# One-hot rows of the second keys stored token by token in the stage that builds the gate table

## The chip, the cores and the metric

The kernel runs on one core of a Trainium2 chip. The metric is the device time of one execution in microseconds (us), lower is better. Engines are named as in the profile: PE (matmuls) and PEld (its weight loads), DVE, ACT, POOL and SP (which only starts DMAs here).

## The reference

One layer of a residual block on 1024 tokens of width 1024, all float32: a mixer (gated delta rule and a linear recurrence), cross attention to 256 memory tokens, and a feed-forward part (PEER) that picks, for every token and each of 8 heads, the 16 best of 128 x 128 experts by the sum of two key scores. Cut to what matters here:

```python
def reference(x, mem, ...):
    x = x + hybrid_mixer(rmsnorm(x, norm_mix_w[0]), ...)
    x = x + memory_cross_attention(rmsnorm(x, norm_xattn_w[0]), rmsnorm(mem, norm_mem_w[0]), ...)
    x = x + peer_ffn(rmsnorm(x, norm_ffn_w[0]), ...)   # 128 (head, rank) slots per token:
    return rmsnorm(x, norm_final_w)                    # first key, second key, gate
```

What the changed stage computes: for each of 512 tokens the 128 x 128 table gate[second key, first key]. A token has 128 slots (8 heads x 16 ranks), each with a first key, a second key and a gate. The table is the product over the slots of the one-hot rows of the second keys with the one-hot rows of the first keys, these multiplied by the gates.

## The kernel before, in words

The tokens are treated in two ways. For 512 of them (D0 = 256 to 767) all 16384 experts are computed densely, and the gate table is multiplied in. For the other 512 each chosen expert's row is fetched from memory by POOL (line 1130) and worked into the token by DVE: 1024 row steps for 4 blocks of 128 tokens, a ring of 6 row buffers (tile `rb`). These steps are put between the other instructions by `Paced`, which counts estimated PE time; so DVE carries a stream of 1.2 us steps all the time.

The program runs in this order: mixers and attention (0 to about 1350 us in the trace), the gate stage (`gates`, from 1352 to 1821 us), and the dense part (from there to the end). The gate stage of the first 256 tokens runs beside the last attention unit and its key search; the order of all instructions on every engine is fixed when the program is written out, by estimates of each engine's time.

Gate stage, lines 942 to 996: the keys and gates of the tokens are transposed into `e1T`, `e2T` and `gtT` ([128 slots, tokens]). `gated(t0)` makes the one-hots of four tokens: DVE writes `o1` (first keys, bf16) and `o2` (second keys, float32, lines 963 and 966); ACT multiplies `o1` by the gates into `og` (tile `ohg`, four instructions). `products` does one float32 matmul per token with `o2` as weights and `og` as the moving operand (line 975; in the profile `gd<-ohg,oh`, two weight loads and two matmuls per token), ACT copies the result to `stage` (line 980) and after 16 tokens starts the DMA of 1 MB to the table `gd` in DRAM. `o2`, `og` and `stage` have two buffers each. The weights of one matmul are read as

```python
o2 = p.tile([128, 128, 4], F, name="oh2", bufs=2)     # [slot, key, token]
pe.matmul(ps[:, t, :], o2[:, :, t], og[:, t, :], start=True, stop=True)
```

so the 128 columns of one token's weights lie 4 floats (16 bytes) apart.

Of the kernel before, what the change touches and what calls it, by code (L numbers as in the profile page):

```python
# [8 lines left out]
F = mybir.dt.float32  # L9
BF = mybir.dt.bfloat16  # L10
FR = mybir.dt.float32r
I32 = mybir.dt.int32
U32 = mybir.dt.uint32
AF = mybir.ActivationFunctionType
# [3 lines left out]
D = 1024  # L18
# [4 lines left out]
D0 = T                      # the tokens that go by all experts; the others go by their experts' rows  # L23
# [26 lines left out]
def block_kernel(ctx: ExitStack, tc: tile.TileContext, a):  # L50
# [3 lines left out]
    written = {}                # by tile: when which part of it is written, by the estimate  # L54
# [17 lines left out]
    class Engine:  # L72
        """An engine, and an estimate of when it is through with what it got so far."""
# [25 lines left out]
    class Paced(Engine):  # L99
        """The tensor engine, with steps of the stream of rows put between its instructions."""  # L100
# [29 lines left out]
    early = gat.tile([128, NROW + 2, D], FR, name="rb")   # until the rows come  # L130
# [9 lines left out]
    # ---------------------------------------------------------------- constants  # L140
    identf = consts.tile([128, 128], F, name="identf")
    identb = fc.tile([128, 128], BF, name="identb")
    triu = fc.tile([128, 128], F, name="triu")          # [t, i] = t <= i
    ones = fc.tile([128, 128], F, name="ones")
    negm = fc.tile([128, 128], BF, name="negm")         # [j, i] = -1e30 where i < j
    iota16 = consts.tile([128, 16], BF, name="iota16")
    # masks of the block recursion: W = (T X) o (I - M_s); M_s[r, c] = 1 where r // s is odd
    # and c // s = r // s - 1 (the first one transposed)
# [53 lines left out]
    lpar = ld("lpar", (128, 4, 4))                          # conv_b, ba, bx, lambda  # L202
# [9 lines left out]
    # ---------------------------------------------------------------- helpers  # L212
    def rsqrt(v, n, name):
        """1/sqrt(v) for a positive [128, n] tile: a bit guess and Newton's steps."""
        ti = small.tile([128, n], I32, name=name + "i")
        y = small.tile([128, n], F, name=name + "y")
        t = small.tile([128, n], F, name=name + "t")
        dve.tensor_scalar(ti, v.bitcast(I32), 1, None, op0=OP.logical_shift_right)
        dve.tensor_scalar(y.bitcast(I32), ti, -1.0, 1597463007.0, op0=OP.mult, op1=OP.add)
        for _ in range(3):  # L220
            dve.tensor_mul(t, y, y)
            dve.scalar_tensor_tensor(t, t, -0.5, v, op0=OP.mult, op1=OP.mult)
            dve.scalar_tensor_tensor(y, t, 1.5, y, op0=OP.add, op1=OP.mult)
        return y

    def softplus(x, n, name):
        """max(x, 0) + log1p(exp(-|x|)), the log by its atanh series."""
        e = small.tile([128, n], F, name=name + "e")
        d = small.tile([128, n], F, name=name + "d")
        z2 = small.tile([128, n], F, name=name + "z")  # L230
        act.activation(e, x, AF.Abs)
        act.activation(e, e, AF.Exp, scale=-1.0)
        dve.tensor_scalar(d, e, 2.0, None, op0=OP.add)
        dve.reciprocal(d, d)
        dve.tensor_mul(e, e, d)
        dve.tensor_mul(z2, e, e)
        dve.tensor_scalar(d, z2, 1.0 / 19.0, None, op0=OP.mult)
        for k in (17, 15, 13, 11, 9, 7, 5, 3):
            dve.scalar_tensor_tensor(d, d, 1.0 / k, z2, op0=OP.add, op1=OP.mult)
        dve.scalar_tensor_tensor(d, d, 1.0, e, op0=OP.add, op1=OP.mult)  # L240
        dve.tensor_scalar(e, x, 0.0, None, op0=OP.max)
        dve.scalar_tensor_tensor(d, d, 2.0, e, op0=OP.mult, op1=OP.add)
        return d
# [8 lines left out]
    def wload(src):  # L252
        """A piece of weights: 1024 rows x 128 columns, [128, 8, 128]."""
        w = wp.tile([128, D], F, name="w", bufs=3)
        sp.dma_start(w, src)
        return c8(w)

    def norm(X, nb, Y, junk):
        """RMS of token-major tiles, to Y."""
# [9 lines left out]
    class Both:  # L269
        """Two tiles [128, 4, T] as one of 8."""  # L270
# [6 lines left out]
    class Pair:  # L277
        """A float32 operand as two float32r parts, for the time in which the gathered rows' memory
        is free; tmp: a place for [128, T] of products."""
# [3 lines left out]
    def low(i):  # L283
        """Memory of the rows, [128, 8, T]."""
        return early[:, 2 * i:2 * i + 2, :].rearrange("p s (c t) -> p (s c) t", c=D // T)

    def transposed(hT, Y, nb, wcol):
        """Token-major tiles to [d, chunk, tok], by the weights."""
# [30 lines left out]
    def proj_T(wname, j, hT, n):  # L319
        """[128 columns, n tokens] of the product with one 128-column tile of weights."""  # L320
# [17 lines left out]
    def proj(wname, j, lhs, nb, b0=0):  # L338
        """The token-major products [128 tokens, nb blocks, 128 columns]."""
# [18 lines left out]
    # ---------------------------------------------------------------- once: masks, gates' constants  # L358
# [18 lines left out]
    # ---------------------------------------------------------------- once: memory keys, values  # L377
# [26 lines left out]
    # ---------------------------------------------------------------- the mixer, T tokens  # L404
# [9 lines left out]
    def mixer(fp, t0, qkv):  # L414
        def conv(ps, ti, w, out, bias=0.0):
            """Causal 4-tap convolution along the tokens of one channel tile."""
# [16 lines left out]
        # a, b: token-major  # L433
# [25 lines left out]
        # q, k, v: channel-major, convolved, silu  # L459
# [12 lines left out]
        def side():  # L472
            # z: token-major, 2 silu(z)
# [8 lines left out]
            # RG-LRU: channel-major  # L482
            for j in range(4):
# [17 lines left out]
                # t = tanh(|log a| / 2): a = (1 - t) / (1 + t), sqrt(1 - a^2) = 2 sqrt(t) / (1 + t);  # L501
                # 1 / (1 + t) = (1 + exp(log a)) / 2, with a step of Newton's
# [6 lines left out]
                dve.scalar_tensor_tensor(rc, nw, 2.0, rc, op0=OP.subtract, op1=OP.mult)     # -1 / (1 + t)  # L509
# [13 lines left out]
        def out(b0, b1):  # L523
            """x1 = x + y W_out of some blocks."""
# [11 lines left out]
        # gated delta rule  # L536
# [17 lines left out]
        def prepare(b):  # L554
            """What a chunk needs of its decays and keys before its own steps."""
# [34 lines left out]
        for b in range(NB):  # L590
# [15 lines left out]
            if b == NB - 1 and t0 + T < S:  # L606
                load_x(qkv, t0 + T)             # keys and values of this pass are done with
# [101 lines left out]
            def normed(b, tok, o, rq):  # L709
                so = small.tile([128, 4], F, name="g_so")  # L710
                sq_sum(o, so)
                # o is short of the factor rq: rms(rq o) = rq o / sqrt(rq^2 mean(o^2) + eps)
# [15 lines left out]
                act.activation(qkv[:, 0:4, tok], py, AF.Copy, scale=gnw)    # q of these tokens is done with  # L728
# [24 lines left out]
    done = {}                           # x1, by its first token  # L753
    read, chosen = set(), set()         # ends of the tokens whose x2 is read, whose experts are chosen

    # ---------------------------------------------------------------- cross attention and keys
    def attend(fp, t0, nb, KT, VM):
# [52 lines left out]
        # PEER's keys  # L810
# [60 lines left out]
    def select(p, keep, s12, i12, row):  # L871
        """The 16 best of each head's sums. A pair (i, j) of the sorted lists can be among
        them only when (i + 1)(j + 1) <= 16; those all lie in: row 0 (16), rows 1-7 (j < 8),
        rows 8-15 (j = 0), kept in the order of the full table."""
# [24 lines left out]
        # position -> (i, j)  # L899
# [6 lines left out]
        dve.tensor_sub(t1, pf, low)                                     # 8 (pos // 8)  # L906
        # j = low, + 8 in the first row's second half, 0 from 72 on
# [3 lines left out]
        # i = max(pos // 8 - 1, 0), + low from 72 on  # L911
# [29 lines left out]
    # ---------------------------------------------------------------- experts, all of them  # L941
    def gates(p, hT):
        """The table of gates, [second key, first key], to DRAM."""
# [3 lines left out]
        # by slot: first key, second key, gate of every token  # L947
# [12 lines left out]
        def gated(t0):  # L960
            """The one-hots of 4 tokens, the first keys' by the gates."""
            o1 = p.tile([128, 128, 4], BF, name="oh1", bufs=2)
            o2 = p.tile([128, 128, 4], F, name="oh2", bufs=2)
            bc = [128, 128, 4]
            dve.tensor_tensor(o1, iot, e1T[:, None, t0:t0 + 4].to_broadcast(bc), op=OP.is_equal)
            dve.tensor_tensor(o2, iot, e2T[:, None, t0:t0 + 4].to_broadcast(bc), op=OP.is_equal)
# [5 lines left out]
        def products(t0, o2, og):  # L972
            ps = bank("gd").rearrange("p (t e) -> p t e", t=4)
            for t in range(4):
                pe.matmul(ps[:, t, :], o2[:, :, t], og[:, t, :], start=True, stop=True)
# [123 lines left out]
    # ---------------------------------------------------------------- experts, by their rows  # L1099
    # a stream of steps, put between the others' instructions: each step fetches a row per token  # L1100
    # (some steps ahead) and works on one that has come
# [74 lines left out]
    def together(*streams):  # L1176
        """Streams of pieces of work. A stream yields how long its next piece has to wait for what
        it gave the other engines to do (None: for another stream), or a stream to go beside it.
        Of those that are ready, the one of the least rank goes on; at the same rank, the one
        that had the least, measured by its share."""  # L1180
# [41 lines left out]
    # ---------------------------------------------------------------- the order of it all  # L1222

    def mixed():
        """The mixers, then the gates of the passes that take all experts."""
# [105 lines left out]
```

## Time and profile before

| what | us |
|---|---|
| median of 3 runs | 3305.86 |
| lowest, highest run | 3297.55, 3307.26 |
| profiled execution, first to last instruction (its span; no other time of it is recorded) | 3300.7 |
| PE busy, weight loads | 3053.8, 2638.8 |
| DVE busy | 2740.9 |
| gate stage, first to last of its work | 1352 to 1821 |

A span is a share of one execution; the runs differ by 9.7 us between them, and the span lies 5.2 us under their median. "Busy" of PE says that a matmul was under way, not that PE ran at its peak, since matmuls overlap. The granted clock of PE is shown as a share of 2.4 GHz; it has two levels, 1.2 and 2.4 GHz, so 0.66 is a mix of both.

### The profile page before, as it was taken

The numbers are of one execution on the slowest core, as the hardware profiler recorded it, in microseconds if no ns is written. First come the engines' busy times: TensorE is split into PE (matmuls) and PEld (weight loads), VectorE is DVE, ScalarE is ACT, GpSimd is POOL, SyncE is SP. The second block draws the span as 40 slices with busy tenths as digits, with TensorE's granted clock in tenths as the row PEclk, the third lists the DMA queues.
The fourth block names the chain that finished last, engine by engine and source line by source line (L and its number), as shares of the span: only waits on it lengthen the run. The fifth ranks groups of instructions, "written<-read, shape, count | busy, mean of one in ns | idle before, by whom it ended". The sixth has DMA issues, their size and how long they took to land.

```text
span 3300.7 us, 46517 instructions
## 1 busy us (share of the span) xinstructions
PE 3053.8 (93%) x16212; PEld 2638.8 (80%) x16212; DVE 2740.9 (83%) x5999; ACT 1282.9 (39%) x2694; POOL 1430.2 (43%) x1045
## 2 busy tenths in 40 slices
PE   7999997698999989999868799999999999999998
PEld 6888887677988878898868677888888878888886
DVE  7634776877787889887899798888999988899998
ACT  6833452236323632465358332222222222222222
POOL 0000233334433343333333475665666665656663
PEclk9999998899999999999868899999999999999999
DMA  4346778688887678778888788999998999899995
GB/s 170 111 145 210 251 279 309 228 290 291 297 298 284 232 259 320 270 265 282 303 279 234 289 326 328 335 335 335 336 333 323 331 337 332 325 345 327 340 333 197
DMA packets 321547, 941.66 MB, mean 285 GB/s; under 512 B 28912, under 2 KB 108832, under 8 KB 319264
## 3 DMA queue, kind: packets, MB, share of 16 engines
q0 software_dynamic: 148048, 538.04, 46.2%
q1 hardware_dynamic: 107216, 367.08, 30.5%
q10 hardware_dynamic: 66048, 33.56, 3.6%
q8 instruction: 128, 2.10, 0.2%
q14 instruction: 107, 0.88, 0.1%
HBM read 894.53 MB, written 44.04 MB: 284 GB/s over the span
## 4 chain that ended last, share of the span: by engine, by line
PE 56%; DVE 14%; DMA 10%; issue 9%; POOL 7%; ACT 4%; SPq 0%; POOLq 0%; ACTq 0%; DVEq 0%
PE pj L106 17%; PE dh L106 15%; PE po L106 14%; PE gd L106 7%; POOL rb L1130 7%; DVE rb L82 4%; DMA rb<-in_u,idx 4%; DVE oh L82 2%; PE sc L106 1%; DMA w<-in_pwq 1%; PE tp L111 1%; DMA gd<-stage 1%; DMA w<-in_wout 1%; DVE cy L82 1%; ACT L82 1%
## 5 line engine op out<-in xcount | busy, mean ns | idle before, releaser
L1130 POOL DMA_INDIRECT rb<-in_u,idx x512 | 682.3, 1333 | 1128.2 <-DVE rb L82 509.6
L1130 POOL DMA_INDIRECT rb<-in_v,idx x512 | 739.1, 1444 | 702.8 <-DVE rb L82 487.8
L82 DVE SCALAR_TENSOR_TENSOR rb<-rb 128x1024 f32<-128x1024 f32 x512 | 614.4, 1220 | 97.8 <-DMA rb<-in_u,idx 97.5
L82 DVE SCALAR_TENSOR_TENSOR rb<-rb,ga 128x1024 f32<-128x1024 f32 x512 | 655.6, 1280 | 12.5 <-DMA rb<-in_v,idx 6.1
L106 PE MATMUL pj<-hT,w 128*128 128x256 f32 (+1 forms) x2880 | 592.5, 358 | 18.0 <-DMA w<-in_pwq 12.8
L106 PEld LDWEIGHTS pj<-hT,w 128*128 128x128 f32 x2880 | 493.9, 196 | 75.8 <-DMA w<-in_pwq 13.7
L106 PE MATMUL dh<-hT_h,uh 128*128 128x512 f32 x1024 | 407.5, 398 | 17.8 <-ACT dg L82 17.1
L106 PE MATMUL po<-vh,dah 128*128 128x512 f32 x1024 | 404.7, 395 | 8.9 <-DVE acc L82 7.6
L106 PE MATMUL dh<-hT_l,uh 128*128 128x512 f32 x1024 | 406.4, 397 | 0.0
L106 PE MATMUL dh<-hT_h,ul 128*128 128x512 f32 x1024 | 406.3, 397 | 0.0
L106 PE MATMUL po<-vh,dal 128*128 128x512 f32 x1024 | 405.1, 396 | 0.4 <-DVE dal L82 0.4
L106 PE MATMUL po<-vl,dah 128*128 128x512 f32 x1024 | 405.1, 396 | 0.0
L82 ACT CAST uh<-ur 128x1024 fp32r<-128x1024 f32 x128 | 134.7, 1052 | 551.8 <-PE dh L106 363.5
L106 PE MATMUL gd<-ohg,oh 128*128 128x128 f32 x1024 | 254.7, 409 | 47.2 <-ACT ohg L82 28.6
L106 PEld LDWEIGHTS gd<-ohg,oh 128*128 128x128 f32 x1024 | 245.9, 328 | 56.3 <-ACT ohg L82 42.1
L106 PEld LDWEIGHTS dh<-hT_h,uh 128*128 128x128 f32 x1024 | 193.4, 189 | 65.8 <-ACT dg L82 18.0
L106 PEld LDWEIGHTS po<-vh,dah 128*128 128x128 f32 x1024 | 192.1, 188 | 57.8 <-DVE acc L82 9.3
L106 PEld LDWEIGHTS dh<-hT_h,ul 128*128 128x128 f32 x1024 | 193.1, 189 | 47.1
L106 PEld LDWEIGHTS dh<-hT_l,uh 128*128 128x128 f32 x1024 | 193.4, 189 | 46.5
L106 PEld LDWEIGHTS po<-vl,dah 128*128 128x128 f32 x1024 | 192.2, 188 | 47.2
L106 PEld LDWEIGHTS po<-vh,dal 128*128 128x128 f32 x1024 | 192.2, 188 | 47.0 <-DVE dal L82 0.8
L82 ACT CAST dah<-dg 128x512 fp32r<-128x512 f32 x128 | 79.5, 621 | 301.0 <-DVE dg L82 301.0
(338 smaller groups left out, 4836.2 us busy)
## 6 DMA issues: line engine op xcount, KB each, us to landing
ur<-in_ut SPq DMA_DIRECT2D x128, 512.0 KB
vr<-in_v SPq DMA_DIRECT2D x128, 512.0 KB
w<-in_wA SPq DMA_DIRECT2D x80, 512.0 KB
w<-in_pwq SPq DMA_DIRECT2D x80, 512.0 KB
gd<-stage ACTq DMA_DIRECT2D x32, 1024.0 KB
G<-gd SPq DMA_DIRECT2D x16, 2048.0 KB
w<-in_wout SPq DMA_DIRECT2D x40, 512.0 KB
w<-in_wq SPq DMA_DIRECT2D x40, 512.0 KB
```

The lines of the kernel that those rows point to most:

```text
L82: r = call(*args, **kw)
L106: self.engine.matmul(out, l, r, **kw)
L111: self.engine.transpose(out, i, ident)
L1130: pool.indirect_dma_start(out=t, out_offset=None, in_=a[ph], in_offset=bass.IndirectOffsetOnAxis(ap=B["idx"][:, k:k + 1], axis=0))
```

## The change

`o2` is laid out [slot, token, key] instead of [slot, key, token]: the 128 columns of one token's weights now lie side by side. To write it so, DVE compares another constant, `keys` ([128 slots, 128 keys], each row 0 to 127), read again for each of the four tokens, with `e2T`, each of whose values is read 128 times. The old constant `iot` stays for the first keys. One instruction of POOL is new, the one that fills `keys`.

```diff
+        keys = p.tile([128, 128], BF, name="keys", bufs=1)
+        pool.iota(keys, pattern=[[1, 128]], base=0, channel_multiplier=0,
+                  allow_small_or_imprecise_dtypes=True)
...
-            o2 = p.tile([128, 128, 4], F, name="oh2", bufs=2)
-            bc = [128, 128, 4]
+            o2 = p.tile([128, 4, 128], F, name="oh2", bufs=2)
+            bc, tb = [128, 128, 4], [128, 4, 128]
             dve.tensor_tensor(o1, iot, e1T[:, None, t0:t0 + 4].to_broadcast(bc), op=OP.is_equal)
-            dve.tensor_tensor(o2, iot, e2T[:, None, t0:t0 + 4].to_broadcast(bc), op=OP.is_equal)
+            dve.tensor_tensor(o2, keys[:, None, :].to_broadcast(tb),
+                              e2T[:, t0:t0 + 4, None].to_broadcast(tb), op=OP.is_equal)
...
-                pe.matmul(ps[:, t, :], o2[:, :, t], og[:, t, :], start=True, stop=True)
+                pe.matmul(ps[:, t, :], o2[:, t, :], og[:, t, :], start=True, stop=True)
```

The instructions of every engine stand in the same order as before. Two places differ. On POOL, at the start of the gate stage, between the fetches of rows; before:

```order
L1130 DMA rb<-in_u,idx 128x1024 [waits DMASW3_49,DVE_49]
L945 IOTA iot 128x512 [waits DMAHW1_49,DMAHW2_49,DMAHW0_49,DMAHW3_49,PE_49,DMAHW7_49,Activation_49,Pool_49]
L1130 DMA rb<-in_u,idx 128x1024 [waits DMASW4_49,DVE_49]
L1130 DMA rb<-in_u,idx 128x1024 [waits DMASW5_49,DVE_49]
L1130 DMA rb<-in_u,idx 128x1024 [waits DMASW6_49,DVE_49]
```

and now:

```order
L1134 DMA rb<-in_u,idx 128x1024 [waits DMASW3_49,DVE_49]
L945 IOTA iot 128x512 [waits DMAHW1_49,DMAHW2_49,DMAHW0_49,DMAHW3_49,PE_49,DMAHW7_49,Activation_49,Pool_49]
L948 IOTA keys 128x128
L1134 DMA rb<-in_u,idx 128x1024 [waits DMASW4_49,DVE_49]
L1134 DMA rb<-in_u,idx 128x1024 [waits DMASW5_49,DVE_49]
```

The new instruction stands right behind the old one, and the later fetches of rows move one place back. On DVE at the first two groups of four tokens (`e1T`, `e2T` the keys by slot, `X` the residual, `hT_l` a part of the dense operand); before:

```order
L82 TENSOR_TENSOR X_11571<-X_11571,pj 128x2x128 [waits PE_49]
L82 TENSOR_TENSOR oh_11806<-iot,e1T 128x512 [waits Activation_49,Pool_49]
L82 TENSOR_TENSOR oh_11807<-iot,e2T 128x512 [waits Activation_49]
L82 TENSOR_TENSOR oh_11815<-iot,e1T 128x512
L82 TENSOR_TENSOR oh_11816<-iot,e2T 128x512
L82 TENSOR_TENSOR oh_11863<-iot,e1T 128x512 [waits DVE_49,Activation_49]
```

and now:

```order
L82 TENSOR_TENSOR X_11571<-X_11571,pj 128x2x128 [waits PE_49]
L82 TENSOR_TENSOR oh_11808<-iot,e1T 128x512 [waits Activation_49,Pool_49]
L82 TENSOR_TENSOR oh_11809<-keys,e2T 128x512 [waits Activation_49,Pool_49]
L82 TENSOR_TENSOR oh_11817<-iot,e1T 128x512
L82 TENSOR_TENSOR oh_11818<-keys,e2T 128x512
L82 TENSOR_TENSOR oh_11865<-iot,e1T 128x512 [waits DVE_49,Activation_49]
```

The first one-hot of second keys now waits for POOL too; nothing changed its place.

## Rows read from the trace of the kernel before

**Rows 1.** The page: the chain that ended last, shares by engine and line.

```profile
PE pj L106 17%; PE dh L106 15%; PE po L106 14%; PE gd L106 7%; POOL rb L1130 7%; DVE rb L82 4%; DMA rb<-in_u,idx 4%; DVE oh L82 2%; PE sc L106 1%; DMA w<-in_pwq 1%; PE tp L111 1%; DMA gd<-stage 1%; DMA w<-in_wout 1%; DVE cy L82 1%; ACT L82 1%
```

**Rows 2.** Stretches: length, busy us by engine, granted clock, DMA share, GB/s.

```profile
1352.00:1660.00 308.00, 287.75 (x1440) 267.71 (x1440) 260.32 (x852) 172.19 (x462) 101.18 (x84) 0.93 0.82 276
1660.00:1764.00 104.00, 70.37 (x280) 65.78 (x278) 98.47 (x321) 61.30 (x166) 38.23 (x29) 0.66 0.84 266
1764.00:1821.00 57.00, 54.98 (x233) 54.44 (x233) 50.33 (x82) 52.20 (x147) 25.01 (x16) 0.94 0.91 262
1960.00:3250.00 1290.00, 1281.71 (x5483) 1029.43 (x5482) 1169.30 (x1383) 365.82 (x464) 799.44 (x525) 1.00 0.91 332
```

**Rows 3.** The chain that ended last within 1352 to 1660 us, shares by line.

```profile
by line: PE pj L106 33.3%; PE gd L106 26.6%; DVE oh L82 7.8%; DMA rb<-in_u,idx 5.9%; DVE rb L82 5.8%; PE sc L106 4.3%; issue 2.9%; DMA subk<-in_subk 2.5%; PE tp L111 1.9%; DVE i L82 1.2%; POOL rb L1130 1.1%; DVE s L82 0.8%; ACT oT L82 0.7%;
```

**Rows 4.** The products alone by stretch: us, busy PE, PEld, ACT, clock, DMA share, GB/s.

```profile
1352.00:1660.00 308.00, 132.88 (x528) 128.42 (x528) 89.63 (x268) 0.93 0.82 276
...
1764.00:1821.00 57.00, 54.97 (x232) 54.42 (x232) 38.98 (x116) 0.94 0.91 262
```

**Rows 5.** Tile gd: weight loads, ns min/median/max, first and last start.

```profile
L106 PEld LDWEIGHTS gd<-ohg,oh x1024: 307/329/338, 1359.2 to 1819.8; 128*128 128x128 f32 x171
L106 PEld LDWEIGHTS gd<-Xi,TT x384: 186/192/333, 89.3 to 1286.9; 128*128 128x128 f32 x192
```

**Rows 6.** Timeline of weight loads, 1529 to 1538 us: start, length, instruction, count.

```profile
1529.84 3.81 PEld L106 LDWEIGHTS gd<-ohg,oh 128*128 128x128 f32 x16
1533.55 3.67 PEld L106 LDWEIGHTS pj<-w,oT 128*128 128x128 f32 x32
```

**Rows 7.** Waits of DVE, 1352 to 1660 us: total us, times, longest.

```profile
DVE oh L82 <- PE gd L106: 19.2, 24, 1.9
DVE rb L82 <- DMA rb<-in_u,idx: 8.3, 5, 3.3
DVE oh L82 <- ACT ohg L82: 7.5, 3, 7.0
DVE X L82 <- PE pj L106: 3.9, 3, 2.0
DVE s L82 <- PE sc L106: 2.5, 1, 2.5
...
DVE oh L82 <- POOL iot L945: 1.0, 1, 1.0
```

**Rows 8.** Price rows: DVE writes of 128x512 float32, and POOL's constant.

```profile
L82 DVE TENSOR_TENSOR oh<-iot,e2T x128: 667/686/742, 1353.8 to 1817.2; 128x512 f32<-128x512 bf16 x128
...
L82 DVE TENSOR_TENSOR kd<-g,E x8: 682/684/693, 81.1 to 1188.1; 128x512 f32<-128x512 f32 x8
...
L82 DVE TENSOR_TENSOR dg<-dg,G x128: 1071/1192/1230, 1850.4 to 3277.1; 128x512 f32<-128x512 f32 x128
...
L945 POOL IOTA iot<- x1: 1195/1195/1195, 1352.2 to 1352.2; 128x512 bf16 x1
```

**Rows 9.** Waits of DVE, 1764 to 1821 us: total us, times, longest.

```profile
DVE oh L82 <- PE gd L106: 6.5, 11, 0.9
```

**Rows 10.** Timeline of ACT, 1784 to 1793 us, and the chain behind the stage.

```profile
1784.65 1.32 ACT L82 ACTIVATE ohg<-oh,gtT 128x128 f32<-128x128 bf16 x4
1785.96 0.58 ACT L82 COPY stage<-gd 128x512 f32<-128x512 f32 x1
1786.44 1.32 ACT L82 ACTIVATE ohg<-oh,gtT 128x128 f32<-128x128 bf16 x4
1787.83 0.59 ACT L82 COPY stage<-gd 128x512 f32<-128x512 f32 x1
...
1820.96 18.14 DMA gd<-stage
```

**Rows 11.** Matmuls of the projections, 1352 to 1660 us, ns min/median/max.

```profile
L106 PE MATMUL pj<-hT,w x462: 379/379/636, 1351.8 to 1660.0; 128*128 128x256 f32 x154
...
L106 PE MATMUL pj<-w,oT x256: 272/275/422, 1469.7 to 1537.1; 128*128 128x128 f32 x128
```

## The prediction

> **What bounds the kernel now.** I read the page's chain first [rows 1]: the products of the gate stage, with the mixers' products under the same name, hold 7% of it. So the changed matmuls lie on the path that sets the end. Then the table of stretches [rows 2]. It splits the gate stage in three. From 1352 to 1660 us the stage runs beside attention: PE is busy 287.75 of 308 us, DVE 260.32. From 1660 to 1764 DVE is the bound, 98.47 of 104 us, with PE at 70.37. From 1764 to 1821 PE does little but these products, and ACT is nearly as full as PE: 52.20 against 54.98 of 57 us. Behind it, from 1960 on, the dense part keeps PE busy 1281.71 of 1290 us, so time gained ahead of it shifts all of it and is not lost again. What is to be seen: PE is first in only one of three stretches, the longest, and there DVE is close behind, with 308 - 260.3 = 47.7 us of idle time.
>
> **The change, part by part.**
>
> *Weight loads.* The load of the one-hot weights takes 329 ns at the median, that of a like operand whose columns lie side by side 192 [rows 5]. Durations overlap, so the pace counts. Sixteen loads in a row take 3.81 us: (3.81 - 0.33) / 15 = 0.232 us each. Thirty-two of the projection next to them, also 128 columns of float32 with 128 moving columns, take 3.67: (3.67 - 0.19) / 31 = 0.112 [rows 6]. The change turns the first kind into the second: 0.120 us for each of 1024, 123 us of PE time. That is work, not time gained. The first stretch holds 528 of them, the last 232 [rows 4], so 264 stand between; I go through the stretches in turn.
>
> *1352 to 1660.* 528 x 0.120 = 63 us of PE work go. The chain within the stretch [rows 3] gives the products 26.6%, 82 us; brought to 0.112 / 0.232 of that, they would give up 42 us. That is the upper end if nothing takes PE's place. But DVE does: its order is fixed and it can only save what it now waits. Its waits that hang on PE's progress are 19.2 us (a buffer of second-key one-hots not yet free), 3.9 (a projection behind such products) and 2.5 (key scores), 25.6 us together [rows 7]. The 8.3 us for fetched rows and the 7.5 for ACT stay. I take 25.6. The lower end: as the stretch gets shorter, the same bytes must pass in less time. At 276 GB/s over 308 us that is 85 MB; in 282 us it is 301 GB/s, below the 332 that the dense part moves [rows 2], so DMA should carry it, with some more waits for rows. If those and the clock (below) give back more than half, 10 us remain.
>
> *1660 to 1764.* DVE is idle for 104 - 98.5 = 5.5 us in all [rows 2], whatever it waits for. 0 to 5.5, taken as 0.
>
> *1764 to 1821.* PE needs 8 x 0.232 = 1.86 us for four tokens, and the copies to the stage follow at 1787.83 - 1785.96 = 1.87. But ACT's own work for four tokens is from 1784.65 to 1786.44, 1.79 us without a gap [rows 10]. So 0.08 us for each of 29 groups, 2 us at most, although 6.5 us of DVE's waits [rows 9] stand there: what PE frees, ACT takes over. Taken as 1. The DMA of the last 16 tokens behind it, 18.14 us on the chain [rows 10], stays.
>
> *The DVE compare.* It writes 512 float32 values as before, now contiguous by token, with one operand that repeats each value 128 times. The nearest row is the one of the same shape whose second operand is also repeated 128 times, float32 there: 684 ns, against 686 for the compare now. The far end is a multiply that reads float32 values 32 bytes apart, 1192 [rows 8]. I take no change. The far end would cost 128 x 0.506 = 65 us of DVE time, which I hold for a small chance, since the new operands have no such step. A price below 0.67 us stands in no row of a 512-wide float32 write.
>
> *The new constant.* POOL's fill of 512 columns takes 1.195 us [rows 8]; a quarter of the columns costs 0.3 to 1.2. DVE waited 1.0 us for the old one [rows 7]. The new one runs while DVE does its first compare of first keys, and fetches of rows queue behind it on POOL, which is busy 101 of 308 us. 0 to 1 us, taken as 0.6.
>
> Sum: 25.6 + 0 + 1 - 0.6 = 26 us off the span of 3300.7. The span lies 5.2 us under the median of the runs and inside their spread, so I take 26 off the median: 3305.9 - 26 = **3280 us**, 0.8%.
>
> **A rule against it.** The rows show two loads of 128 float32 columns at 329 and 192 ns [rows 5], and the pace goes with them [rows 6]. The Trainium skill, "TensorE: Matmul & The Clock Gate", section "LDWEIGHTS (loading the stationary operand)", makes a load's time a matter of its column count alone, and its section "Step-by-step: what each phase is for" lets the next load run under the matmul in progress. By that the layout would be free and the sum 0; the two rows disagree, as nothing but the step between columns sets these operands apart by shape and type.
>
> **Rivals.**
>
> *The layout is not the cause.* The pace of 0.232 could come from what the products wait for, two fresh operands per token, or from the moving side. Then the loads stay at their pace and the time at 3306. Against it: the loads themselves are long, 307 ns even at the shortest of 1024 [rows 5], and sixteen in a row without a wait keep the pace.
>
> The Trainium skill, "SBUF — State Buffer", section "Door 1: The DMA port swizzle (why `[64,N]` ≈ `[32,N]`)", says that one can step for free up to 4 fp32 values, which is this operand's step; read so, this rival holds and the time is 3306. The row of 329 against 192 ns [rows 5] speaks for the same note's other half, a price for each access on a new 16-byte line.
>
> *The gain is given back.* DVE stops waiting for PE and waits for rows, weights or ACT instead. For it: DMA at a share of 0.82 already, 8.3 us of such waits [rows 2, 7]. Then 0 to 10 us are gained, 3296 to 3306.
>
> *More than the waits named.* PE's earlier results also let ACT go on, and DVE's waits for ACT go with them. All 47.7 us of DVE's idle time is the limit, 3258; at DVE's share of the second stretch, 98.47 / 104 = 0.947, the first would take 260.3 / 0.947 = 275, which is 33 us off, 3273. Beyond 42 us I give it little.
>
> *Slower: PE's clock.* With less to do and waits between, PE may be granted 1.2 instead of 2.4 GHz in more of the first stretch. The second stretch shows it: 0.66 with PE busy 68% [rows 2]; the first has 0.93 at 93%, and would have (288 - 63) / 282 = 80% after the change. At the low level a projection matmul takes 636 instead of 379 ns, or 422 instead of 275 [rows 11]: 462 x 0.257 + 256 x 0.147 = 156 us if all did. PE's slack after the change is 63 - 26 = 37 us, so the gain starts to shrink when a further 37 / 156 = 24% of the stretch goes slow. It turns to a loss beyond 63 / 156 = 40%. The low share is now 14% (twice 0.07), so 54%, a mean clock of 0.73, decides. At 0.66 the low share is 68%, 54% more than now: 84 - 63 = 21 us slower, 3327. Against it: PE stays on the chain for its projections, and in stretches where it runs dry it is not the bound.
>
> **How the numbers follow.** The forecast (10 to 42 us off) 0.67; more than 42 off 0.05; given back 0.14; layout not the cause 0.05; slower, by the clock or the dearer compare, 0.09. Differences within 0.3%, about 10 us, can't be told from none here. Faster by more than that: 0.67 + 0.05 = 0.72. Within: 0.14 + 0.05 = 0.19. Slower: 0.09. The range runs from 3262 (43 us off: the chain's 42 and 1 of the tail) to 3299 (7 us off, most of the cases that give back); it leaves out the slower 0.09, the 0.05 where nothing changes and a few hundredths at each end.
>
> **What would show it.** Loads of the one-hot weights at 192 ns and their pace near 0.112: the first step. Compares at 0.68 to 0.69 us: the DVE step. In the first stretch DVE's waits for PE's products gone and the stretch some 26 us shorter; if they turn up as waits for rows or ACT, the second rival. The last 57 us within 2 us of now, bound by ACT. A granted clock under 0.8 in the first stretch would point to the last rival. A dense part of another length would make the whole reading wrong.

## The result, and the profile after

| | before | after |
|---|---|---|
| median of 7 runs, us | 3307.26 | 3279.88 |
| lowest, highest | 3294.91, 3315.94 | 3269.96, 3288.18 |
| profiled execution: span | 3300.7 | 3273.7 |
| profiled execution: own time | not recorded | 3275.43 |

The ratio is 0.9919, with a 95% interval of 0.9898 to 0.9939: 27 us less, 0.8%. The forecast was 3280 and 0.8%. Single times spread over some 20 us, so that the forecast and the median agree to 0.1 us is luck.

The instructions stand in the same order, but for POOL's new one, so stretches can be cut at the same instructions in both traces. The first stretch goes from ACT's first copy of transposed keys to the last pair of key scores (1352.07 to 1667.89 us before; the prediction ended it 7 us earlier), the middle on to the first of the last 116 gated one-hots, the tail on to the last copy to the stage. The columns are as in [rows 2]: length, busy time of PE, PEld, DVE, ACT, POOL, granted clock, DMA share, GB/s. Before:

```profile
1352.07:1667.89 315.82, 292.62 (x1462) 272.37 (x1460) 268.17 (x871) 175.47 (x469) 106.69 (x89) 0.93 0.81 273
1667.89:1764.11 96.22, 65.42 (x256) 61.10 (x256) 90.69 (x302) 58.01 (x158) 32.71 (x25) 0.63 0.86 274
1764.11:1820.92 56.81, 54.97 (x232) 54.42 (x232) 50.14 (x81) 52.12 (x147) 24.93 (x16) 0.94 0.91 262
```

After:

```profile
1351.63:1643.10 291.47, 246.44 (x1463) 220.21 (x1462) 264.77 (x871) 171.92 (x469) 107.11 (x90) 0.91 0.87 296
1643.10:1736.89 93.79, 55.84 (x256) 49.97 (x256) 90.44 (x302) 58.06 (x158) 35.96 (x25) 0.66 0.87 280
1736.89:1789.83 52.94, 42.00 (x232) 35.76 (x232) 49.87 (x81) 50.50 (x147) 26.04 (x16) 0.94 0.92 275
```

The first stretch is 24.4 us shorter, the middle 2.4, the tail 3.9; the start is 0.4 earlier and all that follows takes 1483.9 instead of 1479.8, 4.1 more. Together 27.0. In the first stretch PE lost 46 us of busy time and DVE 3: PE went from 93% busy to 85%, DVE from 85% to 91%. Over the three stretches PE lost 69 us (413.0 to 344.3).

The operations themselves (tile of the one-hots; ns minimum, median, maximum), to be set beside [rows 5] and [rows 8]:

```profile
L106 PEld LDWEIGHTS gd<-ohg,oh x1024: 186/192/338, 1358.8 to 1788.8; 128*128 128x128 f32 x171
...
L82 DVE TENSOR_TENSOR oh<-keys,e2T x128: 628/682/740, 1353.3 to 1786.5; 128x512 f32<-128x512 bf16 x128
```

That median hides the middle stretch, where the granted clock is 0.66 and most of the new loads are no shorter than the 329 ns of before (in the two other stretches the medians are 192 and 189):

```profile
L106 PEld LDWEIGHTS gd<-ohg,oh x248: 186/333/338, 1646.6 to 1733.7; 128*128 128x128 f32 x124
```

DVE's waits in the first stretch after, beside [rows 7]:

```profile
DVE oh L82 <- ACT ohg L82: 10.8, 4, 5.9
DVE rb L82 <- DMA rb<-in_u,idx: 8.8, 4, 4.2
DVE X L82 <- PE pj L106: 2.0, 1, 2.0
```

The wait for PE's products, 19.2 us, is down to 0.6, that behind key scores is gone, and the projection's went from 3.9 to 2.0. With PE's smaller rows, DVE waited 26.0 us for PE before and 2.6 after. The waits for rows stayed, the one for ACT grew by 3. The chain within the stretch, beside [rows 3]:

```profile
by line: DVE rb L82 23.5%; DVE oh L82 19.8%; DMA gd<-stage 8.4%; DMA rb<-in_u,idx 6.5%; DVE i L82 5.7%; issue 4.9%; PE pj L106 4.4%; DVE s L82 4.2%; DVE mr L82 3.7%; DMA hT_l<-hTd 2.0%; DVE pos L82 1.7%; PE gd L106 1.7%; ACT ohg L82 1.2%; P
```

PE's two lines had 60% of it and have 6%; DVE has taken their place.

### The profile page after: what moved, and what is told of

Read it like the earlier page. It is cut to its first block, busy times and chain, and to the rows that moved or that the text cites. A ratio compares the mean times of both kernels' runs of the same rounds, so it can differ in the third digit from the quotient of the medians.

```text
span 3273.7 us, 46519 instructions
## 1 busy us (share of the span) xinstructions
PE 2987.4 (91%) x16212; PEld 2559.6 (78%) x16212; DVE 2737.6 (84%) x5999; ACT 1277.8 (39%) x2694; POOL 1431.4 (44%) x1046
## 3 DMA queue, kind: packets, MB, share of 16 engines
q10 hardware_dynamic: 66048, 33.56, 3.7%
## 4 chain that ended last, share of the span: by engine, by line
PE 61%; DVE 20%; DMA 9%; ACT 5%; issue 3%; POOL 1%; SPq 0%; ACTq 0%; DVEq 0%; POOLq 0%
PE dh L106 21%; PE po L106 20%; PE pj L106 15%; DVE rb L82 6%; DMA rb<-in_u,idx 4%; PE gd L106 3%; DVE oh L82 3%; DMA gd<-stage 2%; DMA w<-in_pwq 1%; PE tp L111 1%; PE sc L106 1%; DVE cy L82 1%; ACT ohg L82 1%; DVE i L82 1%; ACT L82 1%
## 5 line engine op out<-in xcount | busy, mean ns | idle before, releaser
L106 PE MATMUL pj<-hT,w 128*128 128x256 f32 (+1 forms) x2880 | 590.6, 358 | 16.2 <-DMA w<-in_pwq 11.8
L106 PE MATMUL gd<-ohg,oh 128*128 128x128 f32 x1024 | 183.7, 332 | 81.4 <-ACT ohg L82 54.5
L106 PEld LDWEIGHTS gd<-ohg,oh 128*128 128x128 f32 x1024 | 163.8, 228 | 101.9 <-ACT ohg L82 80.5
L82 DVE TENSOR_TENSOR ul<-ur,uh 128x1024 fp32r<-128x1024 f32 x128 | 156.0, 1222 | 48.7 <-ACT uh L82 27.6
```

The source lines that it names most:

```text
L82: r = call(*args, **kw)
L106: self.engine.matmul(out, l, r, **kw)
```

## The experiments

All kernels below keep the order of the changed kernel where nothing else is said. Total times scatter by some 10 us, and two places where the scatter lies can be named: the start of the stage moves between 1346 and 1360 us though nothing changed ahead of it, and the rest behind it between 1480 and 1488 (less in the two kernels with a fuller DVE, which have another order). So the lengths of the stretches, from one profile each, are set beside the times. Among kernels of one layout the first stretch differs by 2.5 us, the middle by 5. The last column is DVE's wait for PE in the first stretch.

| kernel | first | middle | tail | rest | DVE for PE |
|---|---|---|---|---|---|
| before | 315.8 | 96.2 | 56.8 | 1479.8 | 26.0 |
| after | 291.5 | 93.8 | 52.9 | 1483.9 | 2.6 |
| first half (e1) | 289.2 | 98.8 | 57.2 | 1487.7 | 3.1 |
| second half (e2) | 316.3 | 94.6 | 52.3 | 1484.1 | 27.3 |
| step 2 (e3) | 290.9 | 97.9 | 52.2 | 1484.2 | 3.3 |
| step 8 (e4) | 317.4 | 93.9 | 57.0 | 1481.5 | 26.8 |
| without the constant (e8) | 289.0 | 94.3 | 53.2 | 1483.3 | 2.6 |
| alternate groups (e12) | 299.3 | 95.8 | 54.3 | 1482.0 | 11.4 |
| before, DVE fuller (e5) | 326.7 | 91.1 | 78.3 | 1475.7 | 24.6 |
| after, DVE fuller (e6) | 303.2 | 89.4 | 77.1 | 1472.8 | 2.2 |
| after, one pass (e10) | 287.7 | 94.7 | 52.6 | 1486.8 | 5.2 |

**Where the gain lies: the layout for half of the tokens.**

```diff
-            o2 = p.tile([128, 4, 128], F, name="oh2", bufs=2)
+            o2 = p.tile([128, 4, 128] if t0 < T else [128, 128, 4], F, name="oh2", bufs=2)
...
+            if t0 < T:
                 dve.tensor_tensor(o2, keys[:, None, :].to_broadcast(tb), ...
+            else:
+                dve.tensor_tensor(o2, iot, e2T[:, None, t0:t0 + 4].to_broadcast(bc), op=OP.is_equal)
```

> The new layout for the first 256 tokens of the table only; the other 256 keep the old one. My theory (what counts is the wait of DVE behind PE's products, which lies in the stretch beside attention, where those first 256 tokens are done): nearly the whole gain, 24 to 28 us under the kernel before, first stretch (1352 to 1661 us in the trace of before, 309 us long) near 283 us, the rest of the stage as before (103 and 57 us). Rival (each shorter weight load is worth the same, 27 us over 1024 loads): half, 13 to 14 us. Weight loads: half at 192 ns, half at 329.

Measured: 3283.3 us, ratio 0.9908 (0.988 to 0.9936), 25 us by the medians and 30 by the ratio. The first stretch is as short as after, the tail as long as before.

The other half (`t0 >= T`):

> The new layout for the last 256 tokens only. My theory: PE isn't the bound there, so only the 1 and 4 us that the second stretch and the tail of the stage became shorter, less the 4 us given back behind the stage: 0 to 5 us under the kernel before; first stretch 309 us as before, tail near 53 instead of 57. Rival (each load is worth the same): 13 to 14 us.

Measured: 3303.1 us, ratio 0.9984 (0.9969 to 0.9999), 5 us. The first stretch is as long as before, the tail as short as after. One half is worth all but 5 us. The halves don't save the same, though: in the second one's middle stretch, at a granted clock of 0.63, the new loads take 333 ns at the median, and PE's busy time falls by 21 us in the middle and the tail together, against 43 us in the first stretch of the other kernel. If each saved us of PE counted alike (27 us for 69), that would be 17 and 8 us. The stretches got 26.6 and 6.1 us shorter, and the interval of the first kernel, 21 us or more, leaves 17 out; that of the second, 0 to 10 us, would hold 8. So a load's time has no fixed price: it counts where an engine that sets the pace waits for it.

**What makes the load long: the step between columns.** Two tokens interleaved instead of four, from the changed kernel:

```diff
-            o2 = p.tile([128, 4, 128], F, name="oh2", bufs=2)
-            bc, tb = [128, 128, 4], [128, 4, 128]
+            o2 = p.tile([128, 2, 128, 2], F, name="oh2", bufs=2)
+            bc, tb = [128, 128, 4], [128, 2, 128, 2]
...
-                pe.matmul(ps[:, t, :], o2[:, t, :], og[:, t, :], start=True, stop=True)
+                pe.matmul(ps[:, t, :], o2[:, t // 2, :, t % 2], og[:, t, :], start=True, stop=True)
```

> The one-hots of second keys interleaved by two tokens: the columns of one token's weights lie 2 floats (8 bytes) apart instead of 4 (before) or 1 (after). If the price is one of 16-byte lines that are hit only once, two values a line are enough: loads near 192 ns, pace 0.112 us, time as after, near 3280. If the price grows evenly with the step: 192 + 137 / 3 = 238 ns and a pace near 0.152; the time then between the two, 3285 to 3295, if DVE still waits. DVE's compare at 0.68 to 0.69 us either way by my theory; above 0.8 if its new operands (a value repeated twice inside) cost more.

And the kernel before, padded to eight floats:

```diff
-            o2 = p.tile([128, 128, 4], F, name="oh2", bufs=2)
+            o2 = p.tile([128, 128, 8], F, name="oh2", bufs=2)[:, :, 0:4]
```

> The kernel before with the one-hots of second keys padded: columns 8 floats (32 bytes) apart instead of 4. If each value that lies on a line of its own has one price: loads stay at 329 ns and the time at 3307. If the price grows with the step: 329 + 4 x 46 = 512 ns, a pace near 0.41 us, 184 us more PE work, and 100 to 180 us more in all. DVE writes runs of four floats 32 bytes apart; if that costs it, its compare goes above 0.75 us and adds 128 times the difference where DVE is the bound.

Measured: 3283.6 us with step 2, ratio 0.9918 (0.9901 to 0.9935); 3308.1 with step 8, ratio 1.0003 (0.9989 to 1.0017). The loads with step 2, their pace in a row of sixteen (timeline: start, length, count), and the loads with step 8:

```profile
L106 PEld LDWEIGHTS gd<-ohg,oh x1024: 192/196/337, 1353.7 to 1786.3; 128*128 128x128 f32 x171
```

```profile
1494.83 1.96 PEld L106 LDWEIGHTS gd<-ohg,oh 128*128 128x128 f32 x16
```

```profile
L106 PEld LDWEIGHTS gd<-ohg,oh x1024: 312/335/339, 1361.4 to 1821.4; 128*128 128x128 f32 x171
```

So 192 ns at a step of 1 float, 196 at 2, 329 at 4, 335 at 8; the pace at 2 is (1.96 - 0.20) / 15 = 0.118 us. The price doesn't grow evenly with the step: it appears between 2 and 4 floats and hardly grows from there to 8. One price for every column on a 16-byte line of its own would give that; a step of 3 floats was not run. The layout is the cause, at equal shape, type and order, and DVE's compare costs 0.68 to 0.69 us in all four.

**The constant.** The changed kernel without `keys`:

```diff
-        keys = p.tile([128, 128], BF, name="keys", bufs=1)
...
-            dve.tensor_tensor(o2, keys[:, None, :].to_broadcast(tb),
+            dve.tensor_tensor(o2, iot.rearrange("p k t -> p t k"),
                               e2T[:, t0:t0 + 4, None].to_broadcast(tb), op=OP.is_equal)
```

> The changed layout without the new constant: the compare reads the old constant (bf16) with a step of 4 values instead. Same order but for POOL's one instruction. If the weights' layout alone makes the gain: 3278 to 3285. If a read of bf16 values 8 bytes apart costs DVE something, the compare goes above 0.69 us; at 0.8 that is 14 us of DVE work and about as much lost, 3290 to 3295.

Measured: 3279.6 us, ratio 0.993 (0.9903 to 0.9957), compare 684 ns at the median. The constant and POOL's instruction cost or bring nothing that can be measured, and a read of bf16 values 8 bytes apart costs DVE nothing here.

**Is DVE the next bound, so that a fuller DVE leaves less to gain?**

```diff
+            nc.vector.tensor_tensor(p.tile([128, 128, 4], BF, name="junk", bufs=1), iot,
+                                    e1T[:, None, t0:t0 + 4].to_broadcast(bc), op=OP.is_equal)
             og = p.tile([128, 4, 128], F, name="ohg", bufs=2)
```

Into the kernel before, and into the changed one:

> The kernel before with one more DVE instruction for each group of four tokens, a second compare of first keys into a tile that nobody reads (0.42 us each, 128 of them, 54 us; the instructions of other engines shift a little in their order). It is the base for the next run, which has the same order. By its stretches: 28 us of it fall beside attention, where DVE is idle for 48 of 309 us, 26 in the middle and the tail, where it is nearly full: 25 to 45 us more than before, 3332 to 3352.

> The changed kernel with the same added DVE instruction, in the same order as the run before this one. My theory (the gain is the time in which DVE waited for PE, and DVE is the next bound): with DVE fuller there is less such time, so the change is worth 8 to 18 us here instead of 27. Rival (PE is still what the stage goes by, its saved time counts by itself): 25 to 30 us here as well.

Measured: 3324.2 us, ratio 1.0057 (1.0039 to 1.0076), and 3298.6, ratio 0.9982 (0.9965 to 0.9998). The added work cost 19 us in each, less than I expected, and the change is still worth 25.6 us. My expectation was wrong and the rival's number right. The first stretches tell why. DVE's waits with the added work, before and then after:

```profile
DVE oh L82 <- PE gd L106: 19.0, 21, 1.8
DVE rb L82 <- DMA rb<-in_u,idx: 11.7, 5, 4.4
DVE s L82 <- PE sc L106: 2.6, 2, 1.7
DVE X L82 <- PE pj L106: 2.0, 1, 2.0
```

```profile
DVE rb L82 <- DMA rb<-in_u,idx: 12.5, 6, 4.0
...
DVE X L82 <- PE pj L106: 2.0, 1, 2.0
...
DVE oh L82 <- PE gd L106: 0.2, 1, 0.2
```

I had thought that more work on DVE would eat its waits for PE. They stayed, 24.6 us. DVE's busy time grew by 19.8 us and the stretch by 10.9; of the 7.5 us for ACT [rows 7] only 0.9 are left. The change takes the 24.6 down to 2.2, and the stretch is 23.5 us shorter: the same count as without the added work. (The tail of 77 to 78 us belongs to the other order: 254 DVE instructions lie in it, where the other kernels have some 80.) So the stretch is better seen as sections in a row, some set by PE, others by DVE. The trace of before shows both kinds; these are a section that DVE fills and two that PE fills (columns as above):

```profile
1377.00:1395.00 18.00, 14.13 (x66) 13.10 (x64) 18.00 (x89) 11.55 (x31) 4.93 (x4) 0.87 0.86 276
1395.00:1463.00 68.00, 67.94 (x319) 63.67 (x320) 59.23 (x202) 45.09 (x122) 23.26 (x20) 0.96 0.80 267
1498.00:1543.00 45.00, 44.12 (x289) 43.89 (x288) 37.51 (x116) 22.76 (x62) 16.11 (x14) 1.00 0.96 337
```

In the second and third DVE waits 8.4 and 6.9 us for PE. Work added to DVE lengthens the first kind, a faster PE shortens the other, and the two add up. The sums bear this out; section by section it was not measured.

**Is half of the saving half of the gain?** The new layout for every second group of four tokens (`t0 % 8 == 0` in place of `t0 < T` above):

> The new layout for every second group of four tokens, the old one for the groups between; same order. Half of the saved PE work (31 of 63 us in the stretch beside attention). If the stage is a row of sections, each with its own bound, and DVE is close behind PE in those that PE sets, the first half of the saving is worth more than the second: 16 to 23 us under the kernel before, first stretch 288 to 293 us long. If each saved us counts alike: 13 to 14 us, first stretch 296.

Measured: 3295.6 us, ratio 0.9941 (0.9918 to 0.9965): 15 us by the medians, 19.5 by the ratio, an interval that holds both answers. The first stretch says more: 299.3 us, 16.6 shorter by half of the loads, where all of them give 24.4. (The lengths that I expected, 288 to 293 or 296, were meant from 309 us; they are 21 to 16 or 13 us less.) DVE's waits for PE went from 26.0 to 11.4, 14.6 less. But this half of the loads took 25.8 of the 46.2 us of PE's busy time, more than half; at an equal price per us that is 13.6 us, 3.0 less than the 16.6. With a scatter of 2.5 us, and one profile, of an execution that was 12 us faster than the median of its runs, this points to a first half that is worth more, and doesn't show it.

**Is anything left in PE?** The changed kernel with one pass for the gate products, with operands rounded to float32r (less exact; the order of some products shifts a little):

```diff
-            o2 = p.tile([128, 4, 128], F, name="oh2", bufs=2)
+            o2 = p.tile([128, 4, 128], FR, name="oh2", bufs=2)
...
-            og = p.tile([128, 4, 128], F, name="ohg", bufs=2)
+            og = p.tile([128, 4, 128], FR, name="ohg", bufs=2)
```

> The changed kernel with the gate products in one pass (float32r operands, the gates rounded; less exact): one matmul per token instead of two, so a further 40 to 60 us less PE work in the stage. The order of some products shifts a little. If PE's products are off the path after the change (1.7% of the chain beside attention): 0 to 5 us less than the changed kernel, 3275 to 3282. If a saved us of PE work is still worth what it was (27 per 123): 10 to 13 us less, 3267 to 3270.

Measured: 3279.8 us, ratio 0.9886 (0.9857 to 0.9916); 0.1 us from the changed kernel by the medians, though by the ratios, each to its own runs of before, it could be 11. Its first stretch (columns as above):

```profile
1360.03:1647.77 287.74, 231.63 (x1191) 196.73 (x1189) 264.99 (x871) 172.16 (x469) 109.43 (x90) 0.87 0.88 299
```

That is 3.7 us shorter than after, with a granted clock of 0.87 instead of 0.91 and PE at 80%. The middle is 0.9 us longer and the tail 0.3 shorter, both at a clock of 0.50. Half of the products' instructions are gone, but only 15 us of PE's busy time here and 32 in the whole stage, less than the 40 to 60 expected, and the stretches show little gain. DVE still waits 5.2 us for PE here, so PE is nearly off the path.

**Two tries at a faster version.** After the change the stage's transfers hold 8.4% of the chain in the first stretch. Half-size transfers with four buffers:

```diff
-                stage[0] = p.tile([128, NC, 16, EC], F, name="stage", bufs=2)
+                stage[0] = p.tile([128, NC, 8, EC], F, name="stage", bufs=4)
...
-            if at == 12:
-                act.dma_start(gd[:, :, t0 - 12:t0 + 4, :].rearrange("c e t k -> e c t k"), stage[0])
+            if at == 4:
+                act.dma_start(gd[:, :, t0 - 4:t0 + 4, :].rearrange("c e t k -> e c t k"), stage[0])
```

> The changed kernel with the stage to DRAM cut in 8 tokens by four buffers instead of 16 by two: transfers of half a megabyte in runs of 256 bytes, twice as many, started by ACT as before. The order of instructions shifts. If the wait of ACT for a free stage buffer (13.7 us in the changed kernel) and the 21.7 us behind the last one come from the size of a transfer: 5 to 15 us less than the changed kernel, 3265 to 3275. If the shorter runs make DMA slower or the 32 further starts on ACT (0.4 us each) cost as much: 3280 to 3295.

Measured: 3298.6 us, ratio 0.9983 (0.9968 to 0.9999), 19 us slower than after. Its first stretch:

```profile
1348.74:1655.70 306.96, 250.64 (x1462) 226.16 (x1463) 268.15 (x871) 174.46 (x469) 101.53 (x90) 0.88 0.91 281
```

DMA is busier than after (0.91 against 0.87) and moves less (281 against 296 GB/s): the queue of the stage took 4.6% of the DMA engines' time over the execution, against 3.7% after, for the same 33.56 MB in twice as many packets. DVE waits 15.6 us for ACT there and 11.8 for PE, of which 8.3 for the products. That the shorter runs caused the loss is likely and not shown: the shifted order may have a share, and the two were not separated. The last transfer landed after 17.56 us, though half as large, against 17.8 to 21.7 for the full size in the kernels above; so most of its delay isn't its size.

The transfers started by SP (`sp.dma_start` in place of `act.dma_start` in the changed kernel):

> The changed kernel with the transfers of the stage started by SP instead of ACT (0.37 us each on ACT, 32 of them). The order shifts. If ACT's own work sets the tail (1.67 us for four tokens and the starts between): tail 50 instead of 53 us, and 3 to 10 us less in all, 3270 to 3277. If SP's loads of weights queue behind the waits for the stage: PE waits for weights and the time is 3285 or more.

Measured: 3277.1 us, ratio 0.9886 (0.9859 to 0.9913). It beats the kernel before; against the changed one, 2.8 us by the medians is too little to tell from none. The first stretch is 287.5 us, 4 less than after, and the tail 53.5, not the 50 that I had expected if the starts on ACT set it. The middle is:

```profile
1644.49:1724.40 79.91, 51.23 (x256) 45.25 (x256) 70.75 (x143) 56.96 (x158) 45.12 (x25) 0.72 0.94 306
```

DVE has 143 instructions there instead of 302: the shifted order moved the others behind the stage, where the rest is longer, 1498.3 instead of 1483.9. 14 us went and 14 came back, so this time is no proof of either expectation.

## Why the prediction was right, point by point

*The loads.* Right at the full clock: 192 ns, and the step is the cause. The rival that something else sets the pace falls with the steps of 2 and 8. Too large was the sum of 123 us of PE time, 63 in the first stretch: it gave every load the saving of a full row at the full clock. PE's busy time fell by 69 us, 46 of them in the first stretch, and the 248 new loads of the middle have a median of 333 ns. The forecast didn't suffer, since it was built on DVE's waits and not on that sum.

The Trainium skill, "TensorE: Matmul & The Clock Gate", section "LDWEIGHTS (loading the stationary operand)", gives the time by the number of columns alone; the runs here disagree, with 192 to 335 ns at 128 columns. The Trainium skill, "SBUF — State Buffer", section "Door 1: The DMA port swizzle (why `[64,N]` ≈ `[32,N]`)", has lines of 16 bytes that want two accesses each; the runs agree with that (196 ns at 8 bytes, 329 at 16), and disagree with its free step of 4 fp32 values.

*The first stretch.* Right in kind and size: 25.6 us taken, 25.7 measured up to the end that the prediction used (1660.94 before, 1634.79 after), 24.4 to the later mark. The experiments bear out the count by DVE's waits in three pairs of kernels: 23.4 us of waits gone and 24.4 us shorter; 14.6 and 16.6 with alternate groups; 22.4 and 23.5 with a fuller DVE. The counts agree within some 2 us and not exactly: from before to after DVE's busy time fell by 3.4 us as well, and its other idle time grew by 2.4. The reason I gave with it, that DVE as the next bound limits the gain by its load, was too simple. What limits it is how much of the time DVE really stands behind PE.

*The middle.* 0 taken, from 0 to 5.5; 2.4 measured, and 94 to 99 us in kernels of the new and the old layout alike, so no effect that can be told.

*The tail.* PE was the fullest engine here too, 54.98 of 57 us, so "first in only one of three stretches" was not right. That ACT takes over was right, the size wrong: 1 taken, at most 2; measured 3.9, and in other kernels with the new layout there 3.6 to 4.6 (56.8 less 53.2 to 52.2). The term that was wrong is ACT's own time for four tokens, which I read as 1.79 us in [rows 10], too long, so that too little seemed left to gain. ACT's timeline after:

```profile
1759.99 0.57 ACT L82 COPY stage<-gd 128x512 f32<-128x512 f32 x1
1760.45 1.31 ACT L82 ACTIVATE ohg<-oh,gtT 128x128 f32<-128x128 bf16 x4
1761.66 0.56 ACT L82 COPY stage<-gd 128x512 f32<-128x512 f32 x1
```

From copy to copy 1.67 us. The copy starts 1.21 us after the first of the four, while the fourth is still recorded as running. In [rows 10] it starts 1.31 and 1.39 after, so a small wait for PE lay in the row that I took for ACT without a gap. The same tail before has groups without such a wait, outside that row:

```profile
1794.66 0.57 ACT L82 COPY stage<-gd 128x512 f32<-128x512 f32 x1
1795.13 1.32 ACT L82 ACTIVATE ohg<-oh,gtT 128x128 f32<-128x128 bf16 x4
1796.34 0.57 ACT L82 COPY stage<-gd 128x512 f32<-128x512 f32 x1
```

That is 1.68 us from copy to copy with the old layout. With it the upper end is 29 x (1.87 - 1.67) = 5.8 us, less for the groups that already went at 1.68 or wait for other things.

*The compare and the constant.* Right, nothing: 682 ns against 686, and no difference without the constant. POOL's new instruction took 0.243 us, a little under the 0.3 to 1.2 that I had bounded it by.

*Given back.* DVE's waits for rows stayed, 8.8 us against 8.3, though DMA rose from 273 to 296 GB/s in the first stretch. ACT waited once, 7.7 us, for a transfer of the stage, and DVE's wait for ACT grew from 7.5 to 10.8 us, but it is 7.0 to 8.8 in three other kernels with the new layout there (e1, e3, e8). So the rival with DMA or ACT as the new wait came in a small part at most. The rest behind the stage was 4.1 us longer in the profiled execution, 3.6 of them in the last transfer to the table, 21.73 us instead of 18.14 [rows 10]:

```profile
1789.85 21.73 DMA gd<-stage
```

In the other kernels that keep the order it took 17.8 to 20.5 us in one execution each, in the one of step 8, with the old pace, 18.7. In the table the whole rest is 1482.0 to 1487.7 us in the kernels with new loads and 1479.8 and 1481.5 in the two without (before, step 8), but with a fuller DVE the new layout has the shorter rest, 1472.8 against 1475.7. Whether the 4 us are scatter or an effect stays open.

*The total.* 26 us were forecast and 27 came, and that the sum came so close is partly luck: the middle and the tail gave 5.3 us more than it had for them, and the rest behind the stage took 4.1 that it didn't have.

*The clock.* The mean granted clock of the first stretch went from 0.93 to 0.91, far from the 0.73 at which the rival would have turned the result. Its turning points were nearer than the prediction had them, since PE's busy time fell by 46 us and not by 63: the slack was 46 - 24 = 22 us, not 37. With one pass the first stretch had 0.87 and the tail 0.50, and neither was longer than after, though with less work for PE.

## What to carry to other kernels

Read a gain off the waits of the engine that is second, not off the work that is saved: PE's busy time beside attention fell by 46 us, and 24 us of time followed, which is about what DVE had waited for PE there. Keep the 128 columns of a float32 weight load at most 2 floats apart: the loads here take 196 ns so, and 329 at 4, as long as PE has its full clock. A stretch with two engines close together can be read as a row of sections, each with its own bound.

## What the runs showed of the hardware that I had not expected

A step of two floats between weight columns is nearly free (196 against 192 ns), and a step of eight costs hardly more than one of four (335 against 329).

A row of slow loads, with their matmuls between, takes the same time at both levels of PE's clock; a row of quick ones doesn't. The timeline of weight loads before, eight at a granted clock of 1.00 (1504 to 1508 us) and eight at 0.50, which is 1.2 GHz (1685 to 1695):

```profile
1505.30 1.94 PEld L106 LDWEIGHTS gd<-ohg,oh 128*128 128x128 f32 x8
...
1688.56 1.94 PEld L106 LDWEIGHTS gd<-ohg,oh 128*128 128x128 f32 x8 [1.39 <-ACT ohg L82]
```

And after, at 1.00 (1634 to 1637) and at 0.50 (1656 to 1661):

```profile
1634.79 0.97 PEld L106 LDWEIGHTS gd<-ohg,oh 128*128 128x128 f32 x8
...
1656.85 1.78 PEld L106 LDWEIGHTS gd<-ohg,oh 128*128 128x128 f32 x8 [4.82 <-ACT ohg L82]
```

0.97 us for eight against 1.78. At 1.2 GHz the layout saves only 0.16 of 1.94 us. In the middle stretch, with a mean clock of 0.63 before and 0.66 after, PE's busy time fell by 9.6 us, where 248 loads at the paces of the full clock would give 30.
